# Column sums of an 8192 x 8192 matrix: own semaphores in one critical section, VectorE for all but the last block, a narrower last strip

## The chip, the cores and the metric

The kernel runs on one core of a Trainium2 chip. The metric is the device time of that core in microseconds (us). "Before" and "after" were run on the same chip, in turn. The profiled execution of the kernel before (628.64 us) is not among its six timed ones.

## The reference

```python
x = np.random.randn(8192, 8192).astype(np.float32)

def reference(x):
    return np.sum(x, axis=0)
```

268.44 MB are read and 8192 sums are written. There is almost no arithmetic per byte.

## The kernel before

The rows are cut into 32 blocks of 256 rows (128 partitions x 2 rows, 8 MB). VectorE keeps a running sum over the first 30 blocks. TensorE, with a matrix of ones, sums over the partitions: first the running sum, then both rows of the next-to-last block ("near"), then both rows of the last block, which comes in strips so that little work is left when the last bytes land. A framework places all semaphores.

```python
STRIPS = [[(2048, 4), (2048, 4)], [(2048, 4)], [(1024, 4)], [(512, 4)], [(512, 4)]]
...
    def column_sums(src, piece, start, stop):
        _, c0, w, nj, n, ps, _ = piece
        for j in range(nj):
            nc.tensor.matmul(out=ps[32 * j : 32 * j + 32, :], lhsT=ones,
                             rhs=src[:, c0 + j * n : c0 + (j + 1) * n], ...)
    prev = None
    for t in range(n_blocks - 2):
        xt = load_pool.tile([P, K, C], F32, tag="xt")       # 3 buffers
        nc.sync.dma_start(out=xt, in_=xr[t])
        a, b = xt[:, 0], xt[:, 1]
        if prev is not None:
            nc.vector.tensor_tensor(out=a, in0=a, in1=prev[:, 1], op=ADD)
        nc.vector.tensor_tensor(out=b, in0=b, in1=a, op=ADD)
        prev = xt
    # ... loads of near, and of last in five strips ...
    for piece in pieces: column_sums(prev[:, 1], piece, True, False)
    for piece in pieces:
        for k in range(K): column_sums(near[:, k], piece, False, False)
    for piece in pieces:
        for k in range(K): column_sums(last[:, k], piece, False, k == K - 1)
        nc.vector.tensor_copy(out=res[0:rows, :], in_=ps[0:rows, :])
        eng = nc.scalar if s == len(STRIPS) - 1 else nc.sync
        eng.dma_start(out=out[c0 : c0 + w]..., in_=res[0 : 32 * (nj - 1) + 1 : 32, :])
```

Of the kernel before, what the change touches and what calls it, by code (L numbers as in the profile page):

```python
# [1 line left out]

# [4 lines left out]

F32 = mybir.dt.float32
ADD = mybir.AluOpType.add





STRIPS = [
    [(2048, 4), (2048, 4)],
    [(2048, 4)],
    [(1024, 4)],
    [(512, 4)],
    [(512, 4)],  # L20
]


@with_exitstack
def kernel(
    ctx: ExitStack,
    tc: tile.TileContext,
    x: bass.AP,
    out: bass.AP,
):  # L30
    nc = tc.nc
    P = nc.NUM_PARTITIONS
    R, C = x.shape
    K = 2
    assert R % (P * K) == 0
    assert sum(w for s in STRIPS for w, _ in s) == C
    n_blocks = R // (P * K)

    xr = x.rearrange("(b p k) c -> b p k c", p=P, k=K)

    const_pool = ctx.enter_context(tc.tile_pool(name="const", bufs=1))
    load_pool = ctx.enter_context(tc.tile_pool(name="loads", bufs=3))
    psum_pool = ctx.enter_context(
        tc.tile_pool(name="psum", bufs=1, space=bass.MemoryType.PSUM)
    )

    ones = const_pool.tile([P, 32], F32)
    nc.gpsimd.memset(ones, 1.0)  # L48

    pieces = []  # L50
    c0 = 0
    for s, strip in enumerate(STRIPS):
        for w, nj in strip:
            n = w // nj
            i = len(pieces)
            ps = psum_pool.tile([P, n], F32, name=f"ps{i}", tag=f"ps{i}")
            res = const_pool.tile([P, n], F32, name=f"res{i}", tag=f"res{i}")
            pieces.append((s, c0, w, nj, n, ps, res))
            c0 += w

    def column_sums(src, piece, start, stop):
        _, c0, w, nj, n, ps, _ = piece
        for j in range(nj):
            nc.tensor.matmul(  # L64
                out=ps[32 * j : 32 * j + 32, :],
                lhsT=ones,
                rhs=src[:, c0 + j * n : c0 + (j + 1) * n],
                start=start,
                stop=stop,
                skip_group_check=True,  # L70
            )



    prev = None
    for t in range(n_blocks - 2):
        xt = load_pool.tile([P, K, C], F32, tag="xt")
        nc.sync.dma_start(out=xt, in_=xr[t])  # L78
        a, b = xt[:, 0], xt[:, 1]
        if prev is not None:  # L80
            nc.vector.tensor_tensor(out=a, in0=a, in1=prev[:, 1], op=ADD)  # L81
        nc.vector.tensor_tensor(out=b, in0=b, in1=a, op=ADD)  # L82
        prev = xt


    near = load_pool.tile([P, K, C], F32, tag="xt")
    nc.sync.dma_start(out=near, in_=xr[n_blocks - 2])
    last = load_pool.tile([P, K, C], F32, tag="xt")
    t = n_blocks - 1
    c = 0  # L90
    for strip in STRIPS:
        w = sum(w for w, _ in strip)
        nc.sync.dma_start(out=last[:, :, c : c + w], in_=xr[t][:, :, c : c + w])  # L93
        c += w

    for piece in pieces:
        column_sums(prev[:, 1], piece, True, False)
    for piece in pieces:
        for k in range(K):
            column_sums(near[:, k], piece, False, False)  # L100
    for piece in pieces:
        s, c0, w, nj, n, ps, res = piece
        for k in range(K):
            column_sums(last[:, k], piece, False, k == K - 1)
        rows = 32 * nj
        nc.vector.tensor_copy(out=res[0:rows, :], in_=ps[0:rows, :])  # L106
        eng = nc.scalar if s == len(STRIPS) - 1 else nc.sync
        eng.dma_start(
            out=out[c0 : c0 + w].rearrange("(j i) -> j i", j=nj),
            in_=res[0 : 32 * (nj - 1) + 1 : 32, :],  # L110
        )


# [1 line left out]
_INS = ['x']  # L115
_OUTS = [((8192,), 'float32')]


# [23 lines left out]
```

## Time and profile before

| | before |
|---|---|
| median time (6 executions) | 629.18 us |
| span of the profiled execution | 626.8 us |
| load queue busy, share of 16 DMA engines | 99.1% |
| VectorE busy | 82% |
| last strip landed / TensorE done / last output landed / end | 623.12 / 623.81 / 625.86 / 626.77 us |

Times inside an execution count from the start of the span. Landings are semaphore events of the trace, which has one for each of the 16 DMA engines; a transfer has landed with the last of them.

From the page of the kernel before: the span, the load queue (packets, MB, share of 16 engines), the queues that carry instructions, and groups of instructions (line, engine, operation, shapes, count | busy us, mean ns | idle us before them and what ended it):

```profile
span 626.8 us, 698 instructions
q1 hardware_dynamic: 5864, 268.47, 99.1%
q8 instruction: 2, 0.03, 0.0%
L81 DVE TENSOR_TENSOR xt<-xt 128x8192 f32<-128x8192 f32 x29 | 252.1, 8692 | 64.7 <-DMA xt<-in_x_dram 64.7
L82 DVE TENSOR_TENSOR xt<-xt 128x8192 f32<-128x8192 f32 x30 | 260.7, 8692 | 23.5 <-DMA xt<-in_x_dram 22.5
L64 PE MATMUL ps<-last,ones 128*32 128x512 f32 (+2 forms) x96 | 7.9, 454 | 1.5 <-DMA last<-in_x_dram 1.5
```

The load queue is busy for 99.1% of the span, and VectorE (DVE) waits for loads before each block (64.7 us over 29 waits, 22.5 us before the first). So only the head and the tail can be won. The timeline of the tail, with start us, duration us, and in brackets the idle time before and its releaser:

```profile
618.21 1.92 PE L64 MATMUL ps<-last,ones 128*32 128x512 f32 x16 [0.20 <-DMA last<-in_x_dram]
...
620.67 1.07 PE L64 MATMUL ps<-last,ones 128*32 128x256 f32 x16 [0.54 <-DMA last<-in_x_dram]
...
621.90 0.65 PE L64 MATMUL ps<-last,ones 128*32 128x128 f32 x16 [0.15 <-DMA last<-in_x_dram]
...
623.17 0.64 PE L64 MATMUL ps<-last,ones 128*32 128x128 f32 x16 [0.62 <-DMA last<-in_x_dram]
623.88 0.29 DVE L106 COPY res<-ps 128x128 f32<-128x128 f32 x1 [0.98 <-PE ps L64]
624.20 1.08 ACTq L108 DMA_DIRECT2D out_dram<-res  x1
```

Each group of TensorE (PE) waits for its strip and is done within 0.7 to 1.9 us: TensorE keeps up with the loads. Note the first line for later: eight 512-column matmuls, which are **16 records** (the trace has 240 records for the kernel's 120 matmuls), took 1.92 us. The clock of this time is in the windows view (busy us and instructions of each engine in a stretch, then granted clock, DMA share, GB/s):

```profile
core 0: us, PE busy (x) PEld busy (x) DVE busy (x) POOL busy (x), PEclk, DMA share, GB/s
615.00:618.00 3.00, 3.00 (x30) 0.67 (x20) 0.69 (x1) 0.00 (x0) 1.00 1.01 419
618.00:621.50 3.50, 2.76 (x35) 0.83 (x32) 1.38 (x2) 0.00 (x0) 1.00 0.98 384
```

TensorE had been busy without a pause since 601 us, and its granted clock (PEclk) is 1.00. So 1.92 us is what 16 such records take at **full** speed.

### The profile page before, as it was taken

To read this page: it belongs to the slowest core of one execution; us is meant where nothing else is said; L and a number is where in the kernel's file an instruction comes from. 1 tells how busy PE (TensorE), PEld (TensorE's weight loads), DVE (VectorE), ACT (ScalarE), POOL (GpSimd) and SP (SyncE) were. 2 spreads that over 40 slices of the span, in tenths; PEclk is the share of its full clock that TensorE was granted. 3 is DMA by queue.
4 is the path that set the end of the run, shared out by engine and by line. 5 is a ranking of instruction groups with operands and counts; after the bars stand their busy time and mean duration, and the time that the engine had idled before them with its cause. 6 is when DMAs were issued, how large, how long until landed. Compare 5 with 4: busy or idle time off the path is not lost.

```text
span 626.8 us, 698 instructions
## 1 busy us (share of the span) xinstructions
PE 21.1 (3%) x240; PEld 7.8 (1%) x240; DVE 515.9 (82%) x65; POOL 0.3 (0%) x5
## 2 busy tenths in 40 slices
PE   0000000000000000000000000000000000000067
PEld 0000000000000000000000000000000000000022
DVE  0538988889988889888898888988889988889831
POOL 0000000000000000000000000000000000000000
PEclk9999999999999999999999999999999999999999
DMA  9999999999999999999999999999999999999996
GB/s 402 406 464 402 468 402 468 402 468 402 468 402 468 402 468 402 468 402 468 402 468 402 468 402 468 402 461 410 448 422 435 435 422 448 422 448 422 448 400 273
DMA packets 5876, 268.52 MB, mean 428 GB/s; under 512 B 600, under 2 KB 612, under 8 KB 1392
## 3 DMA queue, kind: packets, MB, share of 16 engines
q1 hardware_dynamic: 5864, 268.47, 99.1%
q8 instruction: 2, 0.03, 0.0%
q14 instruction: 2, 0.02, 0.0%
q10 hardware_dynamic: 8, 0.00, 0.0%
HBM read 268.44 MB, written 0.03 MB: 428 GB/s over the span
## 4 chain that ended last, share of the span: by engine, by line
DMA 78%; DVE 21%; SPq 0%; issue 0%; PE 0%; DVEq 0%
DMA xt<-in_x_dram 73%; DVE xt L81 21%; DMA last<-in_x_dram 4%; SPq L93 0%; PE ps L64 0%; SPq L78 0%; DVEq L81 0%; DVE res L106 0%
## 5 line engine op out<-in xcount | busy, mean ns | idle before, releaser
L81 DVE TENSOR_TENSOR xt<-xt 128x8192 f32<-128x8192 f32 x29 | 252.1, 8692 | 64.7 <-DMA xt<-in_x_dram 64.7
L82 DVE TENSOR_TENSOR xt<-xt 128x8192 f32<-128x8192 f32 x30 | 260.7, 8692 | 23.5 <-DMA xt<-in_x_dram 22.5
L64 PE MATMUL ps<-xt,ones 128*32 128x512 f32 (+2 forms) x48 | 6.5, 719 | 601.1 <-DVE xt L82 601.1
L106 DVE COPY res<-ps 128x512 f32<-128x512 f32 (+2 forms) x6 | 3.1, 514 | 20.0 <-PE ps L64 20.0
L64 PEld LDWEIGHTS ps<-xt,ones 128*32 128x32 f32 x48 | 2.1, 154 | 605.3 <-issue 605.3
L64 PE MATMUL ps<-last,ones 128*32 128x512 f32 (+2 forms) x96 | 7.9, 454 | 1.5 <-DMA last<-in_x_dram 1.5
L64 PE MATMUL ps<-near,ones 128*32 128x512 f32 (+2 forms) x96 | 7.1, 450 | 0.0
L64 PEld LDWEIGHTS ps<-near,ones 128*32 128x32 f32 x96 | 3.0, 110 | 3.9 <-issue 3.5
L64 PEld LDWEIGHTS ps<-last,ones 128*32 128x32 f32 x96 | 2.6, 109 | 6.6 <-DMA last<-in_x_dram 4.1
L48 POOL MEMSET ones<- 128x32 f32 x1 | 0.1, 125 | 0.3 <-POOLq L126 0.3
L126 POOL MEMSET const-bfloat16-1.0<- 128x1 bf16 x1 | 0.1, 102 | 0.0
L126 POOL MEMSET const-uint8-127<- 128x1 uint8 x1 | 0.1, 102 | 0.0
L126 POOL MEMSET const-float32-0.0<- 128x1 f32 x1 | 0.1, 99 | 0.2 <-issue 0.2
L126 POOL MEMSET const-float32-1.0<- 128x1 f32 x1 | 0.1, 99 | 0.0
## 6 DMA issues: line engine op xcount, KB each, us to landing
last<-in_x_dram SPq DMA_DIRECT2D x1, 4096.0 KB
last<-in_x_dram SPq DMA_DIRECT2D x1, 2048.0 KB
last<-in_x_dram SPq DMA_DIRECT2D x1, 1024.0 KB
last<-in_x_dram SPq DMA_DIRECT2D x2, 512.0 KB, 27.8
xt<-in_x_dram SPq DMA_DIRECT2D x30, 29.8
out_dram<-res SPq DMA_DIRECT2D x3, 8.0 KB
near<-in_x_dram SPq DMA_DIRECT2D x1
out_dram<-res SPq DMA_DIRECT2D x1, 4.0 KB
```

The lines of the kernel that those rows point to most:

```text
L48: nc.gpsimd.memset(ones, 1.0)
L64: nc.tensor.matmul(out=ps[32 * j : 32 * j + 32, :], lhsT=ones, rhs=src[:, c0 + j * n : c0 + (j + 1) * n], start=start, stop=stop, skip_gro ...
L81: nc.vector.tensor_tensor(out=a, in0=a, in1=prev[:, 1], op=ADD)
L82: nc.vector.tensor_tensor(out=b, in0=b, in1=a, op=ADD)
L106: nc.vector.tensor_copy(out=res[0:rows, :], in_=ps[0:rows, :])
L126: nc = _bacc.Bacc("TRN2", target_bir_lowering=False, num_devices=1)
```

## The change

The intent: fewer waits and instructions, less work for TensorE, and less left to do after the last bytes. VectorE adds all but the last block, so TensorE sums one carried row and the last block (68 matmuls instead of 120). Semaphores are set by hand in one critical section. The last strip has 256 columns instead of 512. The output leaves in three transfers instead of six. Core of the diff, cut:

```diff
+STRIPS = [2048, 2048, 2048, 1024, 768, 256]
...
+    with tc.tile_critical():
+        nc.gpsimd.memset(ones[:], 1.0).then_inc(s_one, 1)
...      # blocks 0..29: the same two adds, waits folded into the instructions
+        b = near % NBUF            # next-to-last block: now VectorE, in pieces
+        for c0, parts in ((0, ((0, 2 * GROUP),)), (2 * GROUP, ((3, GROUP), (2, GROUP)))):
+            d = vadd(rows(near, 0, c0, w), rows(near, 0, c0, w), rows(near - 1, 1, c0, w), ...)
+            for g, gw in parts:
+                v = vadd(rows(near, 1, ...), rows(near, 1, ...), rows(near, 0, ...), s_dve, d)
...      # loads: the same, by SyncE, each waits for the add that frees its buffer
+        strip_sums(0, True)
+        carry_sums(0, False).then_inc(s_pe, 1)
+        strip_sums(1, True)
+        carry_sums(1, False).then_inc(s_pe, 1)
+        strip_sums(2, True)
+        carry_sums(3, True)
+        strip_sums(3, False)
+        carry_sums(2, False).then_inc(s_pe, 1)
+        strip_sums(4, False).then_inc(s_pe, 1)
+        strip_sums(5, False).then_inc(s_pe, 1)
...      # four copies on ScalarE, the last on VectorE; three output transfers
+        nc.sync.wait_ge(s_out, 48)
```

## The prediction

> **What bounds it now.** The loads. The page gives 268.44 MB read at a mean 428 GB/s and the load queue busy for 99.1% of 16 engines' span; mid-run slices stay near 435 GB/s[...]. The bytes alone are thus an estimated 617 of the 626.8 us. VectorE is busy 82%, but the waits view shows its adds waiting 64.7 + 22.5 us for loads: two adds of 8.69 us per block against 19.3 us of transfer. The chain of waits names adds for 21%, yet the next load is queued some 10 us before the one in flight ends; that is a tie. So only about 10 us can move: head and end. In the timeline most DMA engines finish at 621.7 us, but the last two strips land at 621.9 and 623.1; then come 0.69 us of matmuls, 0.29 of copy, 1.08 of issue, the landing and 0.7 of closing barriers.
>
> **What the change does.**
> 1. Mid-run: same 8 MB loads, three buffers, and first add that frees a buffer. 0 us.
> 2. Head: the built order adds a handshake and a branch before the first load: +0.15 us (estimate from semaphore steps of tens of ns in this trace).
> 3. The next-to-last block goes from TensorE (7 us, hidden) to VectorE: three adds of 4096 columns, two of 2048, 3 x 4.4 + 2 x 2.3 = 17.9 us, scaled from 8.69. They start when the block lands (602.9) and end about 621, just before the last strips land. Matmuls fall from 120 to 68, in bursts, where this trace shows 1.92 us for sixteen 512-column records against 0.85 warm: a backlog of up to 0.5 us, +0.2 expected.
> 4. Last strip 512 -> 256 columns: matmuls 0.65 -> 0.43, copy 0.29 -> 0.22: -0.3 us.
> 5. Two DMA engines finish 0.75 and 1.4 us behind the rest; their lags start at instruction transfers near 413 and 612 us. [...] (two 16 KB packets, near TensorE's 200th and 450th instruction). With fewer instructions the one at 612 moves to about 621 and the last goes: -0.4 us, up to -1 with luck.
> 6. Output in three transfers instead of six, the last still alone on the path: 0 us.
> 7. Leaving the critical section adds a round in which SyncE signals and awaits all engines: +0.4 us.
>
> **Sum.** +0.15 + 0.2 - 0.3 - 0.4 + 0.4: about 0. Only items 2, 3, 4, 5, 7 touch the critical path, each under 1 us. I predict 629.0 us, range 628.1 to 629.9; faster by over 2%: 0.005, within 2%: 0.99, slower: 0.005.
>
> **What would show it.** Right: mid-run DMA share unchanged, load queue at 99%; first load issued 0.1 to 0.2 us later; last add ending near 621 us; last matmuls about 0.45 us; more time between the last output's landing and the end. Wrong: gaps between loads; VectorE's last add or earlier matmuls ending over 1 us after the last strip lands (slower); all DMA engines finishing together (faster by over 1 us)[...].
>
> **What would make it wrong.** The sizes in 5 and 7 are guesses within 0.5 us; instruction fetches could fall on one DMA engine and add up; VectorE's waits on its own previous add could push step 3 past the last landing.

The sum is +0.15 + 0.2 - 0.3 - 0.4 + 0.4 = +0.05 us. The 617 us are the author's estimate, 268.44 MB at the 435 GB/s that the page's mid-run slices average; that loads can go no faster was not shown. Item 5 rests on the packets and lags of the trace alone.

## More of the kernel before

A kernel is executed several times; each execution also has a mean granted clock of TensorE. In the first line of the timeline of the tail, eight 512-column matmuls, which are **16 records**, took 1.92 us.

## The result, and the profile after

| | before | after |
|---|---|---|
| executions (us), granted clock 0.999 to 1.0 | 629.30, 629.20, 628.58, 629.16, 628.60, 629.29 | 628.51, 628.87 |
| executions (us), granted clock 0.997 | none | 630.17, 630.71, 630.90, 631.21 |
| median | 629.18 | 630.44 |

The ratio is 1.0017 (95% interval 1.000 to 1.0034): the same within 2%. It is computed as the mean time of one kernel's fast runs over that of the other's of the same rounds, so it is not quite the ratio of the medians. The clock of the six executions of before is not on record; that of the profiled one was 1.0, and in the nine executions of each later batch the kernel before had 0.999 to 1.0.

The times after fall into two groups, 630.75 and 628.69 us on average, and the clock tells them apart. (A mean of 0.997 is what one stretch of 3.413 us at half speed makes of 628 us.) The profiled execution is one of the slower group. Its page, the lines that answer to those of before:

```profile
span 628.4 us, 441 instructions
q1 hardware_dynamic: 6144, 268.47, 98.8%
q8 instruction: 1, 0.02, 0.0%
L70 DVE TENSOR_TENSOR buf<-buf,buf 128x8192 f32<-128x8192 f32 (+1 forms) x31 | 260.9, 8417 | 66.1 <-DMA buf<-in_x_dram 66.1
L94 PE MATMUL ps<-buf,ones 128*32 128x512 f32 (+4 forms) x136 | 14.3, 579 | 610.4 <-DMA buf<-in_x_dram 610.0
```

The loads are as before, and still what VectorE waits for. TensorE has fewer records than before (136 against 240) but a longer mean: 579 ns against 454 on the last block before (these means mix shapes). Its timeline (same columns):

```profile
602.95 4.42 DVE L70 TENSOR_TENSOR buf<-buf,buf 128x4096 f32<-128x4096 f32 x1 [1.90 <-DMA buf<-in_x_dram]
607.40 4.42 DVE L70 TENSOR_TENSOR buf<-buf 128x4096 f32<-128x4096 f32 x1
...
607.88 3.58 PE L94 MATMUL ps<-buf,ones 128*32 128x512 f32 x16 [607.88 <-DMA buf<-in_x_dram]
...
611.88 3.67 PE L94 MATMUL ps<-buf,ones 128*32 128x512 f32 x32 [0.42 <-DVE buf L70]
...
616.20 4.49 DVE L70 TENSOR_TENSOR buf<-buf 128x2048 f32<-128x2048 f32 x2
...
617.66 7.08 PE L94 MATMUL ps<-buf,ones 128*32 128x512 f32 x88 [2.11 <-DMA buf<-in_x_dram]
...
623.93 1.18 ACT L193 COPY res<-ps 128x512 f32<-128x512 f32 x2 [7.73 <-PE ps L94]
624.54 0.68 SPq L202 DMA_DIRECT2D out_dram<-res  x1
624.81 0.23 DVE L197 COPY res<-ps 128x64 f32<-128x64 f32 x1 [4.11 <-PE ps L94]
625.06 1.07 ACTq L212 DMA_DIRECT2D out_dram<-res  x1
```

Read it so. The first burst of TensorE, after a long idle time, needs 3.58 us for 16 records: about half speed, against 1.92 above. (This is read from the records; the trace's first clock record begins only at 611.27 us, and the windows view prints 1.00 where there is none.) Then comes a pause of 2.11 us in which TensorE waits for strip 2. From 617.66 us on it works without a stop until 624.74 us, although the last strip had landed at 622.68. In the kernel before, TensorE was done 0.69 us after the last landing; here 2.06 us. The windows view says why:

```profile
core 0: us, PE busy (x) PEld busy (x) DVE busy (x) ACT busy (x) POOL busy (x), PEclk, DMA share, GB/s
615.00:618.00 3.00, 0.89 (x12) 0.16 (x8) 2.96 (x2) 0.59 (x1) 0.00 (x0) 1.00 0.99 412
618.00:621.50 3.50, 3.50 (x24) 0.94 (x20) 2.69 (x2) 0.00 (x0) 0.00 (x0) 0.51 1.01 403
```

In 615 to 618 us TensorE was busy for 0.89 us of 3; in 618 to 621.5 its granted clock is 0.51. The trace's clock records give the moment: half speed from 618.10 us for 3.413 us. Half speed for 3.4 us loses an estimated 1.7 us of TensorE's time, just where the last strips land.

### The profile page after: what moved, and what is told of

The parts are those of the page before. It is cut to its first block, busy times and chain, and to the rows that moved or that the text cites. A ratio compares the mean times of both kernels' runs of the same rounds, so it can differ in the third digit from the quotient of the medians.

```text
span 628.4 us, 441 instructions
## 1 busy us (share of the span) xinstructions
PE 14.3 (2%) x136; PEld 4.3 (1%) x136; DVE 530.7 (84%) x65; ACT 3.6 (1%) x5; POOL 0.3 (0%) x5
## 3 DMA queue, kind: packets, MB, share of 16 engines
q1 hardware_dynamic: 6144, 268.47, 98.8%
HBM read 268.44 MB, written 0.03 MB: 427 GB/s over the span
## 4 chain that ended last, share of the span: by engine, by line
DMA 77%; DVE 21%; PE 1%; SPq 0%; issue 0%; ACT 0%
DMA buf<-in_x_dram 77%; DVE buf L70 21%; PE ps L94 1%; SPq L157 0%; ACT res L193 0%; SPq L151 0%; SPq L241 0%; SPq L101 0%
## 5 line engine op out<-in xcount | busy, mean ns | idle before, releaser
L70 DVE TENSOR_TENSOR buf<-buf,buf 128x8192 f32<-128x8192 f32 (+1 forms) x31 | 260.9, 8417 | 66.1 <-DMA buf<-in_x_dram 66.1
L70 DVE TENSOR_TENSOR buf<-buf 128x8192 f32<-128x8192 f32 (+2 forms) x33 | 269.7, 8174 | 24.1 <-DMA buf<-in_x_dram 23.0
L94 PE MATMUL ps<-buf,ones 128*32 128x512 f32 (+4 forms) x136 | 14.3, 579 | 610.4 <-DMA buf<-in_x_dram 610.0
L94 PEld LDWEIGHTS ps<-buf,ones 128*32 128x32 f32 x136 | 4.3, 124 | 620.3 <-DMA buf<-in_x_dram 611.6
L193 ACT COPY res<-ps 128x512 f32<-128x512 f32 (+1 forms) x4 | 2.3, 573 | 620.6 <-PE ps L94 620.6
```

The lines of the kernel that those rows point to most:

```text
L70: i = nc.vector.tensor_tensor(out=o, in0=a, in1=b, op=ADD)
L94: i = nc.tensor.matmul(out=o, lhsT=ones[:], rhs=r, start=start, stop=True, skip_group_check=True)
L193: i = nc.scalar.copy(res[:, 512 * g : 512 * g + w], ps[g][:, 0:w])
```

## The experiments

**Theory A.** The excess over the prediction is TensorE's clock: the pause before strip 2 is followed, in most executions, by a window of half speed, and the tail then hangs on TensorE. **Rival B.** It is the critical section: entry, exit and closing waits, paid in every execution. A side question is **theory C**: instruction fetches make a DMA engine late for good (item 5 of the prediction).

The experiments ran in three batches on three chips: e1, e2, e4, e5; then e8 to e11; then e3, e6, e12. The kernel before, run in each, had medians of 629.07, 628.87 and 628.91 us.

### Filling the pause (e1_filler), and its control (e8_filler_at_start)

```diff
+        for _ in range(2):                      # e1: before strip 2; results are not used
+            nc.tensor.matmul(out=ps[5][0:32, :], lhsT=ones[:], rhs=rows(last, 0, 0, 512), ...)
         strip_sums(2, True)
```

```diff
         nc.tensor.wait_ge(s_one, 1)
+        for _ in range(2):                      # e8: at TensorE's start instead
+            nc.tensor.matmul(out=ps[5][0:32, 0:32], lhsT=ones[:], rhs=ones[:], ...)
```

> The change with two throw-away matmuls of 512 columns put into TensorE's pause before strip 2 (about 1.7 us of its 2.1 us pause), nothing else. Theory A (the half-speed window of TensorE's clock, 618.1 to 621.5 us in the profiled run, makes the tail late, and the pause before strip 2 brings that window about): no execution near 630.2 to 631.2 any more, granted clock 0.999 to 1.0 in all of them, median about 628.7 us. Rival B (the excess is head and exit of the critical section, about 0.7 us, paid in every execution): the same two groups as the change, median above 630. A small cost is possible in both: eight more instructions bring TensorE's instruction fetch about 1 us earlier, onto transfers that still run.

Measured: 628.54, 629.02, 629.35, 628.76, 629.25 us, median 629.02, clock 1.0 in all five. The slower group is gone. Before, in the same batch: 629.07. Timeline and windows of the filler run:

```profile
615.73 1.88 PE L185 MATMUL ps<-buf,ones 128*32 128x512 f32 x4
...
617.61 5.50 PE L94 MATMUL ps<-buf,ones 128*32 128x512 f32 x88
...
622.93 0.53 ACT L198 COPY res<-ps 128x448 f32<-128x448 f32 x1 [0.16 <-PE ps L94]
623.18 0.23 DVE L202 COPY res<-ps 128x64 f32<-128x64 f32 x1 [2.54 <-PE ps L94]
623.44 1.08 ACTq L217 DMA_DIRECT2D out_dram<-res  x1
```

```profile
615.00:618.00 3.00, 3.00 (x20) 0.60 (x12) 2.97 (x2) 0.59 (x1) 0.00 (x0) 1.00 0.99 411
618.00:621.50 3.50, 3.50 (x52) 1.41 (x48) 2.64 (x2) 0.00 (x0) 0.00 (x0) 1.00 1.02 404
```

The same 88 records from 617.6 us on take 5.50 us instead of 7.08; 52 TensorE records instead of 24 fall between 618 and 621.5 us. TensorE ends at 623.11 us, 0.47 us after the last landing.

> Control to the filler run: the change with two throw-away matmuls at TensorE's start (at about 1 us, 32 columns) instead of in the pause before strip 2. Same count of instructions, pause not filled. Theory A (the pause of 2.1 us before strip 2 lets the clock go to half speed): most executions again at granted clock 0.997 and 630.2 to 631.2 us, some at 0.999 to 1.0 and about 628.7. If the filler helped by something else than the pause (count of instructions, the spare bank): one group at about 629.

Measured: 631.04, 630.70, 630.60 us at clock 0.997; 629.44 and 629.21 us at 0.999 and 1.0; median 630.60. The same two groups as the change, with the same number of instructions as the filler run. So it is the filled pause that counts. This control is also a second sample of the change itself. Its profiled execution (629.44 us) is one of the fast ones, and shows a pause of 1.94 us with no half speed after it:

```profile
618.52 5.49 PE L94 MATMUL ps<-buf,ones 128*32 128x512 f32 x88 [1.94 <-DMA buf<-in_x_dram]
```

```profile
615.00:618.00 3.00, 1.59 (x16) 0.24 (x8) 2.97 (x2) 0.58 (x1) 0.00 (x0) 1.00 1.00 422
618.00:621.50 3.50, 2.98 (x40) 1.18 (x44) 3.50 (x2) 0.00 (x0) 0.00 (x0) 1.00 1.02 416
```

The 88 records take 5.49 us, and TensorE ends 0.48 us after the last landing. The fast profiled execution of e4 (below) is like it (5.50 us); the slow one of e5 is like the change's (7.08 us, half speed from 618.39 us). So the pause does not bring half speed every time, and the time goes with the half speed. Over all runs, 12 of the 19 executions of the four kernels with the pause open (the change, e4, e5, e8) have a clock of 0.997; of the 30 executions of the six kernels with the filler (e1, e6, e9 to e12) none has. Of these, e9 to e11 ran on the chip of the control.

### TensorE sums the next-to-last block again (e2_near_on_pe)

The section, the strips and the output stay; the nine lines of VectorE's adds go, and TensorE sums the carry and both rows of that block from 601 us on.

> The change with the share of VectorE undone: TensorE sums the next-to-last block and the carry before it, as in the kernel before; critical section, 256-column last strip, output in three transfers stay. Theory A (bursts of TensorE lead to the half-speed window): TensorE is busy from 601 us on without a pause, no half-speed window after 608 us, about 628.5 to 629.2 us in one group. Rival B (critical section): still 630 or more. TensorE's instructions go back to over 400, so the instruction fetch near 612 us returns and one DMA engine ends about 1.3 us late again: last strip at about 623.3 instead of 622.7.

Measured: 629.33 to 629.81 us, median 629.52, clock 0.999 to 1.0 in all five. One group, as A says; B's "630 or more" did not come. TensorE's first burst starts at 601.39 us and has no pause for 16.89 us. The 16 KB instruction packet came back at 613.43 us and the last strip landed at 623.58 us, as expected. That the median is 0.5 us above the filler run fits this later landing (623.58 against 622.64), though 0.33 us of it were there already when the next-to-last block landed (603.20 against 602.87).

### The section paid twice (e4_two_sections)

```diff
+    with tc.tile_critical():
+        nc.gpsimd.memset(res[0:1, 0:1], 0.0)
+
     with tc.tile_critical():
         nc.gpsimd.memset(ones[:], 1.0).then_inc(s_one, 1)
```

> The change with one more critical section, nearly empty, ahead of the other: entry and exit of a section are paid twice. Theory A says one entry and exit cost about 0.25 + 0.45 us: the first load is issued about 0.6 to 0.8 us later and all times rise by as much, in both groups (about 629.3 and 631.2). Rival B (the section is what costs the whole 1.3 us): rises by 1.3 us or more.

Measured: 629.72 and 629.99 us at clock 1.0; 631.38 and 631.64 us at 0.997. The first load is issued at 1.54 us instead of 0.96. Both groups shift by 0.5 to 1.2 us against the groups of the change and of its control, and stay 1.65 us apart. So one more section costs about 0.6 us at the head, and it does not make the two groups. B falls as the cause of the excess.

### No section at all (e10_no_section), and the last columns in two halves (e11_two_halves)

The filler run's work and order, but with the framework's own semaphores (its scheduler was held to the order as written) and five output transfers. The second run lets strip 3 leave early and strips 4 and 5 together.

```diff
-    widths = [512, 512, 512, 7 * NI, NI]          # e10
+    widths = [512, 512, 512, 4 * NI, 4 * NI]      # e11
```

> The same work split and order as the filler run, but with the framework's own semaphores and no critical section (undoes that part of the change); the output leaves in five transfers. Ledger of theory A for the section: entry +0.23 us (first load at 0.96 instead of 0.73), exit +0.45 us (1.28 instead of 0.83 us from the last landing to the end). Expected 629.02 - 0.6 = about 628.4 us, granted clock 0.999 to 1.0 throughout, last strip landing at about 622.4. If the section costs nothing: 629.0.

Measured: 628.93 to 629.43 us, median 628.99, clock 0.999 to 1.0. Not the 628.4 expected: a miss. The first load is issued at 0.73 us, as before, but the end brings nothing: from the landing of the last output to the end of the span it is 1.37 us, against 1.28 in the filler run and 0.91 in the kernel before. The part of my ledger that charged the exit to the section alone is wrong, or is made up by the waits that the framework puts at the end; which of its waits take the time was not tried apart. The landing was not earlier either (622.99).

This run has a semaphore for each transfer, so it shows one thing that the shared one hides. The last strip's output took 2.04 us from issue (623.79) to landing (625.83), though its packets were done by 625.11; strip 3 and 4's transfer, issued 0.06 us later, had landed at 625.45. In the kernel before, the last output took 1.66 us (624.20 to 625.86).

> The run without section, with the last 2048 columns in two PSUM tiles of 1024 columns: strip 3 leaves early, strips 4 and 5 leave together in the last transfer. In the filler run the second transfer (strips 3 and 4) landed at 625.47 us, about 0.4 us after that of the last strip, so the last strip's transfer was not alone on the path. Expected: the last landing about 0.2 us earlier (the final copy grows from 0.23 to 0.42 us), about 628.2 us. If the last landing does not hang on that transfer: 0.2 us slower than the run without section.

Measured: 628.53 to 629.13 us, median 628.94; before in this batch 628.87. The last output took 1.75 us from issue (624.15) to landing (625.90); the other outputs had all landed by 625.01. That is 0.3 us less than in e10, but the copy grew from 0.23 to 0.42 us, and the time did not move by more than the noise. By what e10 shows, my expectation had named the wrong transfer as the late one. What makes the difference is not shown: in both runs, and in the kernel before, another transfer was in flight for part of the time, and the sizes differ too.

### The narrow last strip alone (e3_before_256), and undone (e6_filler_512)

```diff
-    [(512, 4)],            # e3, in the kernel before
-    [(512, 4)],
+    [(768, 4)],
+    [(256, 4)],
```

```diff
-STRIPS = [2048, 2048, 2048, 1024, 768, 256]      # e6, in the filler run
+STRIPS = [2048, 2048, 2048, 1024, 512, 512]
```

> One part of the change alone: the kernel before, with last strips of 768 and 256 columns instead of 512 and 512. As predicted for this part: last matmuls 0.65 to about 0.43 us, last copy 0.29 to about 0.22 us, so about -0.3 us against the kernel before, if the output's landing does not grow. The fetch near 612 us and its late engine stay (last strip at about 623.1). If rows of 256 bytes in the last output land later than rows of 512 bytes (as 2.04 instead of 1.66 us from issue to landing in the run without section could mean), the gain is cancelled: 0 to +0.1 us.

Measured: 629.01 us median against 628.91 for before in the same batch, ratio 1.0001 (0.9989 to 1.0014): nothing gained. The last copy has 64 columns instead of 128 (0.23 us in the filler run against 0.29 in the kernel before), and TensorE was done 0.48 us after the last landing (623.57 to 624.05) instead of 0.69; but in this execution the last landing was 0.45 us later, and the last output took 1.78 us to land.

> The filler run with the last two strips of 512 columns, as before the change: undoes the narrow last strip alone. Expected from its part of the sum: last matmuls and copy about 0.3 us longer, so 629.3 us instead of 629.02; with the narrow strip worth nothing, 629.0.

Measured: 629.40 us median against 629.02 for the filler run, clock 0.999 to 1.0. The difference, 0.38 us, has the expected sign and about the expected size (0.3), but the two were in different batches, and single executions scatter by 0.7 us. So e6 suggests a few tenths of a us for the narrow strip and e3 shows nothing: that it is worth anything is not shown.

### Instruction fetches (e5_60_waits, e9_filler_240_waits)

```diff
-        nc.tensor.wait_ge(s_one, 1)
+        for _ in range(241):                     # e9, in the filler run; e5: 61, in the change
+            nc.tensor.wait_ge(s_one, 1)
```

> The change with 60 more waits that are already met at TensorE's start, where it is idle: no work changes, only TensorE's instruction count before the strips. Theory C (each instruction fetch makes one DMA engine late for good, because the load queue never lets it catch up): the 16 KB packet moves from 621.9 to about 613 to 618 us and the last engine lands the last strip 0.6 to 1 us later, at 623.3 to 623.7 rather than 622.7. Rival D (the late engines have nothing to do with the fetch): packet moves, landing stays at 622.7.

Measured: 630.63, 630.84, 630.25 us at clock 0.997 and 629.31 us at 1.0. The 60 waits became only 30 instructions (471 in the profile against 441 of the change), and in the slow profiled execution the packet came at 621.70 us, after nearly all data. So this run does not decide.

> The filler run (clock steady, so the tail can be compared) with 120 more wait instructions, already met, at TensorE's start. Theory C (an instruction fetch makes one DMA engine late for good): the 16 KB packet [...] moves from 621.5 to about 612 to 616 us, one engine is then 1 to 1.3 us behind (with luck 0.7) and the last strip lands at about 623.3 instead of 622.6; time 629.02 + 0.5 to 0.7 = about 629.6. Rival D (fetches do not matter): packet moves, landing and time stay (622.6, 629.0).

Measured: 630.19, 630.20, 629.54, 629.25, 630.12 us, median 630.12, clock 1.0 in all five. The 16 KB packet came at 617.28 us instead of 621.54 (the 612 to 616 us expected were the author's estimate). In the strips after it two DMA engines trail: the last strip landed on 14 engines by 622.88 us, on the next at 623.46 and on the last at 624.06; in the filler run the last landed at 622.64. Not all of these 1.42 us are the fetch's: the next-to-last block, which lands before it, was already 0.83 us later than in the filler run (603.70 against 602.87). From that landing to the last strip's it is 20.36 us here and 19.77 in the filler run. This stretch sorts the other traces too: it is 19.75 to 19.77 us in all eight whose 16 KB packet came after 621.5 us (the change, e1, e4, e5, e6, e8, e10, e11), and 20.27 to 20.38 in the four that had one between 612 and 618 us (before, e2, e3, e9). So rival D falls and theory C stands: an instruction fetch that falls on the strips makes the last landing 0.5 to 0.6 us later. The median is 1.1 us above the filler run's, which ran on another chip; what the fetch does not explain of it stays open.

### Another try at theory C (e12_two_queues)

```diff
+        else:                                    # from block 17 on
+            tc.keep_in_program_order(nc.scalar.dma_start(out=xt, in_=xr[t]))
```

> The run with two halves (628.94 us), with block 17 and all later loads issued by ScalarE instead of SyncE, so that SyncE no longer comes to the instruction that set off its fetch near 415 us, which left one DMA engine 0.6 to 0.75 us late in all of the runs since. Theory C: no instruction packet between 100 and 615 us, spread of the landings of one block back to 0.4 us, last strip at about 622.4 instead of 623.15, time about 628.3 us. Rival D: spread stays about 1 us without a fetch. Risk: [...] a gap of loads there would show as one longer step between landings near 330 us (+1 us).

Measured: 630.47 to 631.10 us, median 630.82 against 628.91 for before: slower by 0.3%. Missed in both ways. The 8 KB instruction packet still came, at 416.82 us, so SyncE's count of instructions does not set it off; what does was not found. And the last strip landed at 624.87 us, 1.7 us later than in the run it was made from. 1.15 us of that were lost by the landing of the next-to-last block (604.55 against 603.40), the rest in the strips, though the 16 KB packet came only at 623.49 us; the cause was not followed up.

A further variant, with the wait for the outputs moved behind the section, did not build: the framework's scheduler found a deadlock.

## Why the prediction was wrong

Predicted 629.0 us, 628.1 to 629.9; measured 630.44 us median. The class (within 2%) was right. Point by point:

- **Item 1, mid-run: right.** The load queue is busy 98.8% of a longer span, and the next-to-last block landed at 602.92 us against 602.85 before.
- **Item 2, head +0.15 us: right in kind.** The first load is issued at 0.96 us instead of 0.73: +0.23.
- **Item 3, backlog "up to 0.5 us, +0.2 expected": the step that failed.** Two things were missed. First, a misreading: "1.92 us for sixteen 512-column records against 0.85 warm" compares 16 records with 8 (at full clock, weight loads of four records come 0.43 us apart, so eight take about 0.86). Sixteen records take 1.92 us at full clock and 3.58 at half. So the work after strip 2 fills TensorE up to the end even at full clock (5.50 us from 617.61 to 623.11 in the filler run). Second, the pauses were not held against the clock. In the traces of the two kernels the clock records last 3.413, 6.827 and 20.48 us, but for the last of each, which its end cuts; in e5 half speed lasted 3.41 us again (618.39 to 621.80). What sets half speed off is not shown. In the kernel before, TensorE's longest pause between 601 us and its end is 0.62 us. With the change it has one of 2.11 us before strip 2, and with no slack left the half-speed window went straight into the time: in the profiled execution TensorE ends 1.37 us later after the last landing than in the kernel before (2.06 instead of 0.69), 1.59 us later than with the pause filled (0.47). Filling the pause removed the slower group (0 of 5 executions); the control kept it (3 of 5; the change 4 of 6). So the +0.2 us expected was 1.37 in the profiled slow execution.
- **Item 4, last strip -0.3 us: about right** in the parts: in the filler run TensorE is done 0.47 us after the landing, and the copy takes 0.23 us. In whole times it is within the noise.
- **Item 5, fetch -0.4 us: right.** The last strip landed at 622.68 instead of 623.12 us: -0.44. Counted from the landing of the next-to-last block, which takes out what the loads before it differ by, it is 19.76 us instead of 20.27: -0.51. The packet came at 621.89 us; e2, e3 and e9 show what it costs when it comes sooner.
- **Item 6, output 0 us: wrong by some tenths.** Last matmul to landing of the last output: 2.05 us before, 2.36 in the filler run, though the copy is shorter.
- **Item 7, exit +0.4 us: right in size** (landing to end: 0.91 before, 1.29 after), but the section is not needed for it (e10: 1.37).

With full clock the sum was right: 628.51 and 628.87 us for the change, 629.02 for the filler run, against 629.0 predicted. That is partly luck: at full clock the backlog of +0.2 did not come (TensorE ended 0.47 us after the last landing, against 0.43 predicted for the last strip's matmuls alone), and the 0.3 us of item 6, not foreseen, took its place. The gain of less work and fewer instructions is given back by head, output and exit, and the half-speed window then adds 1.3 to 2.1 us in most executions (the two groups' means differ by 2.06 us for the change, 1.65 in e4, 1.26 in e5, 1.45 in e8). Not tried: a direct measure of how short a pause must be; and no version beat the kernel before (best: 628.94 against 628.87).

## What to carry to other kernels

When an engine's work is cut, look at what its pauses do to it: here TensorE, with 68 matmuls instead of 120 and a pause of about 2 us just ahead of the tail, had a clock of 0.997 in 12 of 19 executions, and in none of 30 with the pause filled; two throw-away matmuls repaired it (median 629.02 us against 630.44). Group executions by their granted clock before averaging; the median of 630.44 us hid two groups, 630.75 and 628.69 us. In a kernel bound by loads, count the instructions of each engine near the end: here 120 more of them on TensorE (e9, 569 instructions against 449 in the filler run) brought a 16 KB instruction packet from 621.54 to 617.28 us, onto the strips, and the last strip had landed only with the slowest of the 16 DMA engines, at 624.06 us, where 14 were done by 622.88.

## What stays open

- Which pauses bring half speed. In the profiled execution of the change, TensorE was busy for about 1.3 us (0.86 before its pause of 2.11 us, 0.44 after) of the 3.413 us before half speed (614.69 to 618.10 us); e5 shows the same (1.3 us busy). In the fast execution of the control, a stretch as long around the pause of 1.94 us (616.63 to 620.05 us) had 1.53 us of work, and the clock stayed at 1.00 in 618 to 621.5 us. Whether this parts the two groups is not shown.
- What sets off the 8 KB instruction packet, which came at 413.33 us in the kernel before, at 452.03 with the change, and at 416.82 in e12, where SyncE issued no loads from block 17 on. In the kernel before, with the load queue 99.1% busy, the slowest of the 16 engines landed 0.15 us after the ninth in the block before this packet, 0.99 us in the block after it and still 0.87 us in the load that had landed at 612.62 us.
